# Two-layer trunk on one core: order of the state-space output products, of cross-attention's output halves, and of the first loads

## The chip, the cores and the metric

The kernel runs on one core of one Trainium2 chip. The metric is the device time of one execution in microseconds (us), the median of several. A core has TensorE (PE in the rows; PEld is its weight load), VectorE (DVE), ScalarE (ACT), GpSimd (POOL) and SyncE (SP). Each runs its own list of instructions in order and waits on the others by semaphores. SP only issues transfers here; ScalarE and GpSimd issue some in between their own work (ACTq and POOLq in rows).

## What is computed

A trunk of two layers over 512 positions of width 1024, with RMSNorm before each part and residual sums. Layer 0 mixes by stick-breaking attention and pooling (not touched here), layer 1 by a state-space layer; each layer then attends to 256 memory tokens in 4 heads and ends with a gated MLP. Cut to the two parts that the change moves:

```python
def s5_ssm(u, ...):                      # u = rmsnorm(x) @ ssm_w_in; 64 groups of 16 channels
    bu = einsum(ug, B)                   # 64 complex states per group
    h  = associative_scan(a, bu)         # h_t = a h_{t-1} + bu_t
    y  = Re(einsum(h, C))
    return y + d_skip * u                # then gelu, GLU, residual
def memory_cross_attention(h, mem_n, w_q, w_kv, w_o):
    q = h @ w_q;  k, v = split(mem_n @ w_kv)
    p = softmax(q k / 16)                # 4 heads of 256
    return (p v) @ w_o
```

## The kernel before

Activations stand transposed, as 8 tiles of 128 channels x 512 positions. Every large product is made exact to about float32 by splitting both sides into a high and a low part and adding three products, high x high, low x high and high x low (`mm3`, L207 to L209, or with the roles changed). Weights come as chunks of 256 KB (128 x 512) through a stream W: SP loads a raw chunk (`wr`, L168), ScalarE copies its high part (`wh`, L113), VectorE subtracts the low part (`wl`, L116). There are four buffers each. `W.take()` hands out a chunk and has the next ones converted, up to four in all, the one in use among them; so the two conversions of a chunk stand in the lists of ScalarE and VectorE where the chunk three places before it is taken.

The order of all engines around the change is written out by hand: each list holds the instructions in the order of the program's text.

**Start.** `x_block` loads x in four blocks of 256 columns (512 KB; the first in two halves); `W.load(n)` sees to it that n raw chunks are on their way. x tiles are then transposed one by one (`psx`, L217), normalised (xh on ScalarE L302, xl on VectorE L303), and one `v_step` of 12 matmuls (`psv`) follows each tile with the next chunk: W1 behind tile 2, W2 behind tile 3, W3 behind tile 4. cm is a block of constants; `columns()` reads it and the gain rows behind the last v_step.

**Cross-attention** (`xattn`, once a layer). `q_tile` makes a tile of q, `q_out` scales it and splits it (`xqh`, `xql`), `q_full` does both. `scores(h)` are two psum tiles of 12 matmuls with 256 columns (`pssc`) and the softmax; `turn(h)` transposes the probabilities (`pspt`), `values(h)` multiplies them by v (`pspv`). `o_first(m)` computes the first half of output tile m from the first two heads (`pso`, 12 matmuls, one chunk); NP says for how many tiles this is done early. The weight stream is put in the same order by `xattn_weights`.

**State space** (`ssm`, layer 1). Eight blocks b of 128 channels. Their steps are put in order by lists of names in `seq`:
- `um(b)` the input projection (24 matmuls, two chunks, `psu`); `uo(b)` scales it on VectorE (`su`) and ScalarE issues its store to DRAM (d_u); `sg(b)` is GpSimd's load of it in another layout; `lx(b)` and `ly(b)` GpSimd's loads of the block's matrices (wi, tb and wq, wo; 512 KB each).
- `x1(b)` the input products (8 float32 products of 64 columns, which the trace shows as 16 matmuls, `psX`), on ScalarE two half swaps `xs` and `mub`, on VectorE `sr`, `xs`, `sr` and the scan `gg`.
- `x2(b)` turns the states: two swaps `gsw` on ScalarE, then `gg`, `gsw` and `hb` on VectorE. hb has two buffers.
- `x3(b)` the output products (`psY`, 16 products, 32 matmuls in the trace: wq with sg, wo with hb), gelu on ScalarE (`sy`) and its store (d_y). `yl(b)` loads it back, `x4(b)` splits it (yh on ScalarE, yl on VectorE).
- between them stands work on the memory tokens for the cross-attention: `kk(m)`, a key tile of 48 matmuls with 256 columns in four chunks (`psk`, then kf, kh, kl), and `vs_(q)`, v-steps with two chunks (`psv`, weights wth and wtl).

All psum tiles of these parts come from one pool of eight banks. The order before is one block apart: x1(b), then x3(b-1).

Of the kernel before, what the change touches and what calls it, by code (L numbers as in the profile page):

```python
# [18 lines left out]
KD = D // 128  # L19
# [33 lines left out]
def trunk_kernel(  # L53
# [141 lines left out]
    W = Stream()  # L195
# [662 lines left out]
    def xattn_weights(layer):  # L858
        for m in range(KD):
            W.cols(xa_w_q[layer], m)  # L860
        for k0 in (0, 4):
            for m in range(3):
                W.cols(xa_w_o[layer], m, k0, 4)
        for m in range(3, KD):
            W.cols(xa_w_o[layer], m)


# [31 lines left out]
    kvm = KV(kv0)  # L899
# [15 lines left out]
    with tc.tile_pool(name="rg0", bufs=1, reuse_waits="tile") as rg, tc.manual_schedule():  # L915
# [9 lines left out]
        def x_block():  # L925
            c = len(xb)
            t = rg.tile([128, 4, 256], F32, tag="xb", bufs=4, name="xb")
            src = x[0, :, c * 256:(c + 1) * 256].rearrange("(i p) d -> p i d", p=128)
            if c == 0:
                nc.sync.dma_start(out=t[:, :, 0:128], in_=src[:, :, 0:128])  # L930
                W.load(1)
                nc.sync.dma_start(out=t[:, :, 128:256], in_=src[:, :, 128:256])
            else:
                nc.sync.dma_start(out=t, in_=src)
            xb.append(t)
# [5 lines left out]
        step(6)  # L941
        for c in range(4):
            x_block()
            W.load(c if c > 1 else 1)
        cm = rg.tile([128, C_W - C_K], F32, tag="cm", name="cm")
        nc.sync.dma_start(out=cm, in_=consts[:, C_K:C_W])
        for q in range(1, len(gl)):
# [312 lines left out]
    def xattn(rg, layer, norm, kv, nxt):  # L1260
# [13 lines left out]
        def q_out():  # L1274
            i = len(st["q"])
            f = np_.tile([128, 512], F32, tag="ev", bufs=2, name="qf")
            V.scalar_tensor_tensor(out=f, in0=ps_[i], scalar=1.0 / 16.0, in1=st["rbc"], op0=ALU.mult, op1=ALU.mult)
            a = rg.tile([128, 512], F32R, tag="xq", bufs=8, name="xqh")
            b = rg.tile([128, 512], F32R, tag="xq", bufs=8, name="xql")
            copy_hi(a, f)  # L1280
            sub_lo(b, f, a)
            st["q"].append((a, b))

        def q_full():
            q_tile()
            q_out()
# [47 lines left out]
                sub_lo(b, ps, a)  # L1334
                st["o"].append((a, b))

        NP = 3
        op = {}

        def o_first(m):  # L1340
            op[m] = psA("pso")
            sproj(op[m], st["o"][0:4], last=False)
# [3 lines left out]
        q_tile()  # L1346
        q_out()
        q_out()
        q_out()
        q_full()  # L1350
        scores(0)
        q_full()
        turn(0)
        scores(1)
# [5 lines left out]
        scores(2)  # L1360
        q_full()
        turn(2)
        scores(3)
        values(2)
        o_first(0)
        turn(3)
        o_first(1)
        values(3)
        o_first(2)
        for m in range(KD):  # L1370
            if m < NP:
                sproj(op[m], st["o"][4:8], first=False)
# [247 lines left out]
    def ssm(rg, norm, nxt, kvm):  # L1620
# [101 lines left out]
        with tc.manual_schedule():  # L1722
# [24 lines left out]
                for f in fs:  # L1747
                    f()

            seq(lx(0), kvm.load, um(0), st, um(1), row, uo(0), sg(0), uo(1), sg(1), lx(1), ly(0), um(2), ac(0), uo(2), sg(2), um(3), ac(1), ac(2), ac(3), lx(2), ly(1))  # L1750
            seq(x1(0), x2(0), uo(3), lx(3), ly(2))
            seq(x1(1), um(4), uo(4), x2(1), x3(0), lx(4), ly(3), sg(3), yl(0), kk(0))
            seq(x1(2), um(5), uo(5), x2(2), x3(1), ly(4), sg(4), kk(1), yl(1))
            seq(x1(3), um(6), uo(6), x2(3), x3(2), lx(5), yl(2), sg(5), kk(2))
            seq(x1(4), um(7), uo(7), x2(4), x3(3), lx(6), sg(6), x4(0), yl(3))
            seq(x1(5), ly(5), kk(3), vs_(0), x2(5), x3(4), ly(6), lx(7), sg(7), yl(4), x4(1), vs_(1))
            seq(x1(6), vs_(2), x2(6), x3(5), ly(7), yl(5), x4(2), x4(3), vs_(3))
            seq(x1(7), vs_(4), x2(7), x3(6), yl(6), vs_(5), x4(4), vs_(6), x3(7), yl(7), x4(5), vs_(7), x4(6))
            gps = []
            for i in range(NG1):  # L1760
                ps = psB("psg")
# [93 lines left out]
```

## Time and profile before

| | |
|---|---|
| time, median of 3 runs | 1507.06 us (1506.47 to 1507.28) |
| profiled execution, device time | 1506.5 us |
| its span in the trace | 1504.7 us |
| busy share of TensorE, VectorE, ScalarE, GpSimd | 98%, 68%, 49%, 28% |
| mean granted clock of TensorE | 0.994 |
| share of TensorE in the chain that ended last | 82% |

The span is from the first to the last instruction of the trace; the device time adds what lies around it. In the rows below a time stands first, from the span's start; "x4" counts like instructions in a row, whose duration is then that of all together; in brackets is the idle time of the engine before the row and the engine whose work ended it. The matmuls' ends are modelled, so the distance between two starts tells more than a duration. PEclk is the clock that TensorE was granted, as a share of the full 2.4 GHz.

### The profile page before, as it was taken

The page shows a single profiled execution, that of the slowest core. Times are in us where ns is not written, and L with a number is a line of the kernel's source. Part 1 is how long each engine was busy: PE and PEld are TensorE (multiplying, and loading weights), DVE is VectorE, ACT ScalarE, POOL GpSimd, SP SyncE. Part 2 cuts the span into 40 slices and gives each one's busy share as a digit, 9 for nine tenths or more (in the row PEclk, how much of TensorE's full clock was granted, in tenths as well). Part 3 has the DMA queues.
Part 4 walks back from the last instruction along what each step waited for, and adds up shares of the span by engine and source line. Part 5 has one row for each costly group of instructions (what it writes and reads, how often), then busy time and mean ns, then how long its engine had stood idle before and what let it go on. Part 6 is the DMA issues. An engine that isn't in the chain of part 4 may idle for free.

```text
span 1504.7 us, 21037 instructions
## 1 busy us (share of the span) xinstructions
PE 1480.7 (98%) x7347; PEld 1234.2 (82%) x7347; DVE 1023.4 (68%) x1586; ACT 733.5 (49%) x1303; POOL 420.5 (28%) x844
## 2 busy tenths in 40 slices
PE   8999999999999999999999999999999999999998
PEld 7787888888888887888788988888888888888887
DVE  4776666676588897888765666556667775377754
ACT  5556764344455534555663545434444543244533
POOL 7885429999000013333752120000000000000002
PEclk9999999999999999999999999999999999999999
DMA  6313243423433344444568876332133333333331
GB/s 184 96 46 96 74 142 99 118 92 107 124 100 105 109 158 135 133 121 129 154 187 306 263 252 194 105 102 70 56 92 91 99 93 96 100 98 98 92 118 56
DMA packets 271941, 183.99 MB, mean 122 GB/s; under 512 B 21271, under 2 KB 252763, under 8 KB 271835
## 3 DMA queue, kind: packets, MB, share of 16 engines
q1 hardware_dynamic: 244731, 132.79, 30.3%
q0 software_dynamic: 15872, 42.26, 8.4%
q10 hardware_dynamic: 11232, 7.61, 1.7%
q8 instruction: 57, 0.93, 0.3%
q14 instruction: 49, 0.40, 0.1%
HBM read 156.13 MB, written 24.12 MB: 120 GB/s over the span
## 4 chain that ended last, share of the span: by engine, by line
PE 82%; DVE 5%; issue 4%; POOL 3%; ACT 2%; DMA 2%; SPq 0%; ACTq 0%; DVEq 0%; POOLq 0%
PE psup L207 10%; PE psup L208 9%; PE psup L209 9%; PE psd L207 5%; PE psd L209 5%; PE psd L208 5%; PE pso L208 2%; PE pso L209 2%; PE pso L207 2%; PE psg L208 2%; PE psg L207 2%; PE psg L209 2%; PE psq L207 2%; PE psq L209 2%; PE psq L208 2%
## 5 line engine op out<-in xcount | busy, mean ns | idle before, releaser
L116 DVE TENSOR_TENSOR wl<-wr,wh 128x512 fp32r<-128x512 f32 (+2 forms) x467 | 325.3, 713 | 142.4 <-ACT wh L113 141.6
L113 ACT ACTIVATE wh<-wr 128x512 fp32r<-128x512 f32 (+2 forms) x467 | 280.4, 617 | 254.9 <-PE psup L208 84.5
L207 PE MATMUL psup<-xh,wh 128*128 128x512 f32 x704 | 275.7, 392 | 0.0
L208 PE MATMUL psup<-xl,wh 128*128 128x512 f32 x704 | 274.4, 390 | 0.0
L209 PE MATMUL psup<-xh,wl 128*128 128x512 f32 x704 | 274.1, 389 | 0.0
L1544 POOL TENSOR_TENSOR acc<-acc,sq 128x256 f32<-128x256 f32 x12 | 8.8, 735 | 558.4 <-ACT sq L1542 558.2
L207 PEld LDWEIGHTS psup<-xh,wh 128*128 128x128 f32 x704 | 132.1, 188 | 28.8 <-issue 1.5
L209 PEld LDWEIGHTS psup<-xh,wl 128*128 128x128 f32 x704 | 132.1, 188 | 28.2 <-DVE wl L116 0.3
L208 PEld LDWEIGHTS psup<-xl,wh 128*128 128x128 f32 x704 | 132.2, 188 | 27.1 <-issue 0.2
L207 PE MATMUL psd<-hh,wh 128*128 128x512 f32 x328 | 130.5, 398 | 0.2 <-ACT hh L113 0.2
L209 PE MATMUL psd<-hh,wl 128*128 128x512 f32 x328 | 128.2, 391 | 0.0
L208 PE MATMUL psd<-hl,wh 128*128 128x512 f32 x328 | 127.9, 390 | 0.2 <-DVE hl L116 0.2
L1458 ACT ACTIVATE fc<-fu,ccols 128x512 f32<-128x512 f32 x44 | 36.0, 818 | 93.7 <-DVE fu L1456 93.7
L302 ACT ACTIVATE xh<-xT,gcols 128x512 fp32r<-128x512 f32 x40 | 33.4, 835 | 97.1 <-DVE xT L325 68.9
L207 PEld LDWEIGHTS psd<-hh,wh 128*128 128x128 f32 x328 | 61.6, 188 | 14.8 <-issue 1.5
L209 PEld LDWEIGHTS psd<-hh,wl 128*128 128x128 f32 x328 | 61.5, 188 | 13.6
L208 PEld LDWEIGHTS psd<-hl,wh 128*128 128x128 f32 x328 | 61.6, 188 | 12.9 <-DVE hl L116 0.5
L715 POOL DMA_DIRECT2D tz<-kt x128 | 65.3, 518 | 7.4 <-POOL kt L712 4.7
L303 DVE SCALAR_TENSOR_TENSOR xl<-xT,gcols,xh 128x512 fp32r<-128x512 f32 x40 | 35.0, 874 | 33.6 <-ACT xh L302 33.5
L658 POOL DMA_DIRECT2D d_win<-wi x16 | 8.7, 546 | 155.5 <-ACT wi L655 155.5
L207 PE MATMUL psq<-xh,wh 128*128 128x512 f32 x128 | 51.1, 399 | 0.0
L1403 DVE TENSOR_TENSOR fu<-psup,rbc 128x512 f32<-128x512 f32 x44 | 30.3, 688 | 29.5 <-PE psup L209 28.2
(352 smaller groups left out, 3500.6 us busy)
## 6 DMA issues: line engine op xcount, KB each, us to landing
wr<-in_ffn_w_up_dram SPq DMA_DIRECT2D x176, 256.0 KB, 2.9
wr<-in_ffn_w_down_dram SPq DMA_DIRECT2D x70, 256.0 KB, 2.9
wr<-in_xa_w_kv_dram SPq DMA_DIRECT2D x64, 256.0 KB, 4.5
wr<-in_ab_w_in_dram SPq DMA_DIRECT2D x32, 256.0 KB, 2.9
wr<-in_xa_w_q_dram SPq DMA_DIRECT2D x32, 256.0 KB, 2.9
wr<-in_xa_w_o_dram SPq DMA_DIRECT2D x32, 256.0 KB, 2.8
wr<-in_ssm_w_glu_dram SPq DMA_DIRECT2D x29, 256.0 KB, 2.8
wr<-in_ffn_w_down_dram SPq DMA_DIRECT2D x24, 192.0 KB, 2.6
```

The costliest lines, as they stand in the source:

```text
L113: A.activation(out=o, in_=i, func=AF.Copy)
L116: V.tensor_tensor(out=o, in0=i, in1=hi.bitcast(F32), op=ALU.subtract)
L207: T.matmul(ps, lhsT=lh, rhs=rh, start=first, stop=False)
L208: T.matmul(ps, lhsT=lh, rhs=rl, start=False, stop=False)
L209: T.matmul(ps, lhsT=ll, rhs=rh, start=False, stop=last)
L302: A.activation(out=ho, in_=src, func=AF.Copy, scale=g)
L303: V.scalar_tensor_tensor(out=lo, in0=src, scalar=g, in1=ho.bitcast(F32), op0=ALU.mult, op1=ALU.subtract)
L658: nc.gpsimd.dma_start(out=d_win[b // 2][:, (b % 2) * 512:(b % 2) * 512 + 512], in_=st["w"])
L715: nc.gpsimd.dma_start(out=tzs[b % 2][j:128:8, :, j * 16:128], in_=ktf[:, :, 0:128 - j * 16])
L1403: V.tensor_tensor(out=u, in0=ps, in1=rbc, op=ALU.mult)
L1458: A.activation(out=c, in_=u, func=AF.Identity, scale=cwcol(layer, 2, t), bias=cbcol(layer, t))
L1544: G.tensor_tensor(out=acc[:, sl], in0=acc[:, sl], in1=sq[:, 0:256], op=ALU.add)
```

## The change

Three parts are changed, all of them orders. At the start two chunks more are asked for early: W1 goes ahead of x1, W2 ahead of x2, W3 ahead of x3, and W4 behind it. In cross-attention NP becomes 4, with the weight stream to match; the third q_out moves behind the first scores, and the first o_first stands ahead of the last scores. In the state-space part x3(b-2) stands behind x1(b), um(4) goes between the first two x1, key tile 0 follows x1(1), key tiles 1 to 3 follow um(5) to um(7), and the v-steps stand one place earlier.

```diff
-            for m in range(3):
+            for m in range(4):
                 W.cols(xa_w_o[layer], m, k0, 4)
-        for m in range(3, KD):
+        for m in range(4, KD):
             W.cols(xa_w_o[layer], m)
...
                 W.load(1)
                 nc.sync.dma_start(out=t[:, :, 128:256], in_=src[:, :, 128:256])
+                W.load(2)
...
             x_block()
-            W.load(c if c > 1 else 1)
+            W.load(c + 2 if c < 3 else 4)
...
-        NP = 3
+        NP = 4
...
         q_out()
         q_out()
-        q_out()
         q_full()
         scores(0)
+        q_out()
...
         turn(2)
+        o_first(0)
         scores(3)
         values(2)
-        o_first(0)
+        o_first(1)
         turn(3)
-        o_first(1)
+        o_first(2)
         values(3)
-        o_first(2)
+        o_first(3)
...
-            seq(lx(0), kvm.load, um(0), st, um(1), row, uo(0), sg(0), uo(1), sg(1), lx(1), ly(0), um(2), ac(0), uo(2), sg(2), um(3), ac(1), ac(2), ac(3), lx(2), ly(1))
-            seq(x1(0), x2(0), uo(3), lx(3), ly(2))
-            seq(x1(1), um(4), uo(4), x2(1), x3(0), lx(4), ly(3), sg(3), yl(0), kk(0))
-            seq(x1(2), um(5), uo(5), x2(2), x3(1), ly(4), sg(4), kk(1), yl(1))
-            seq(x1(3), um(6), uo(6), x2(3), x3(2), lx(5), yl(2), sg(5), kk(2))
-            seq(x1(4), um(7), uo(7), x2(4), x3(3), lx(6), sg(6), x4(0), yl(3))
-            seq(x1(5), ly(5), kk(3), vs_(0), x2(5), x3(4), ly(6), lx(7), sg(7), yl(4), x4(1), vs_(1))
-            seq(x1(6), vs_(2), x2(6), x3(5), ly(7), yl(5), x4(2), x4(3), vs_(3))
-            seq(x1(7), vs_(4), x2(7), x3(6), yl(6), vs_(5), x4(4), vs_(6), x3(7), yl(7), x4(5), vs_(7), x4(6))
+            seq(lx(0), kvm.load, um(0), st, um(1), row, uo(0), sg(0), uo(1), sg(1), lx(1), ly(0), um(2), ac(0), uo(2), sg(2), um(3), ac(1), ac(2), ac(3), lx(2))
+            seq(x1(0), um(4), uo(3), x2(0), ly(1), uo(4), lx(3))
+            seq(x1(1), kk(0), x2(1), ly(2), lx(4))
+            seq(x1(2), x3(0), sg(3), um(5), uo(5), x2(2), ly(3), yl(0), kk(1))
+            seq(x1(3), x3(1), sg(4), um(6), uo(6), x2(3), ly(4), lx(5), yl(1), kk(2))
+            seq(x1(4), x3(2), sg(5), um(7), uo(7), x2(4), lx(6), yl(2), x4(0), kk(3))
+            seq(x1(5), x3(3), sg(6), vs_(0), x2(5), ly(5), lx(7), yl(3), x4(1), vs_(1), vs_(2))
+            seq(x1(6), x3(4), sg(7), vs_(3), x2(6), ly(6), yl(4), x4(2), vs_(4), x4(3))
+            seq(x1(7), x3(5), vs_(5), x2(7), ly(7), yl(5), x3(6), x4(4), yl(6), vs_(6), x3(7), yl(7), x4(5), vs_(7), x4(6))
```

**SP at the start of the program, before** (xb are the x blocks, wr the weight chunks W0, W1, W2, cm constants; the number behind a name tells buffers apart):

```order
L937 DMA cs_76<-in_consts_dram 128x192
L930 DMA xb_232<-in_x_dram 128x4x128
L168 DMA wr_234<-in_ab_w_in_dram 128x512
L932 DMA xb_232<-in_x_dram 128x4x128
L934 DMA xb_237<-in_x_dram 128x4x256
L934 DMA xb_239<-in_x_dram 128x4x256
L168 DMA wr_241<-in_ab_w_in_dram 128x512
L934 DMA xb_243<-in_x_dram 128x4x256
L168 DMA wr_245<-in_ab_w_in_dram 128x512
L946 DMA cm_247<-in_consts_dram 128x640
```

The same place after:

```order
L938 DMA cs_76<-in_consts_dram 128x192
L930 DMA xb_232<-in_x_dram 128x4x128
L168 DMA wr_234<-in_ab_w_in_dram 128x512
L932 DMA xb_232<-in_x_dram 128x4x128
L168 DMA wr_237<-in_ab_w_in_dram 128x512
L935 DMA xb_239<-in_x_dram 128x4x256
L168 DMA wr_241<-in_ab_w_in_dram 128x512
L935 DMA xb_243<-in_x_dram 128x4x256
L168 DMA wr_245<-in_ab_w_in_dram 128x512
L935 DMA xb_247<-in_x_dram 128x4x256
L947 DMA cm_249<-in_consts_dram 128x640
```

W1 stood behind x2 and W2 behind x3, W3 behind all that is shown; now a chunk goes ahead of each of the blocks x1, x2 and x3.

**TensorE in the cross-attention of layer 0, where the last head's scores begin, before** (pspt are the transposes of turn(2), pssc the scores):

```order
L217 MATMUL pspt_4156<-cs_76,p_4076 128x128 x2
L217 MATMUL pspt_4156<-cs_76,p_4095 128x128 x2
L207 MATMUL pssc_4165<-kh_1896,xqh_4034 128x256
L208 MATMUL pssc_4165<-kl_1897,xqh_4034 128x256
L209 MATMUL pssc_4165<-kh_1896,xql_4035 128x256
```

After (pso is the first half of output tile 0; its 12 matmuls begin behind the same transposes, the last three are shown):

```order
L207 MATMUL pso_4165<-oh_4056,wh_4014 128x512
L208 MATMUL pso_4165<-ol_4057,wh_4014 128x512
L209 MATMUL pso_4165<-oh_4056,wl_4015 128x512
L207 MATMUL pssc_4184<-kh_1896,xqh_4034 128x256
L208 MATMUL pssc_4184<-kl_1897,xqh_4034 128x256
L209 MATMUL pssc_4184<-kh_1896,xql_4035 128x256
```

A first half of the output, which came behind values(2), now stands between turn(2) and the scores.

**VectorE in the state-space part, before: from x2(0) to su(4)** (the first three rows are x2(0), the su rows uo(3) and uo(4), the four rows behind the first su x1(1); the wl rows are the low parts of key tile 0's second and third chunk):

```order
L1693 TENSOR_TENSOR gg_8661<-gg_8661,tb_8386 128x512
L1694 TENSOR_TENSOR gsw_8663<-gsw_8663,tb_8386 128x512
L1695 TENSOR_TENSOR hb_8376<-gg_8661,gsw_8663 128x8x64
L1660 TENSOR_TENSOR su_8669<-psu_8564,rbc_8491 128x512
L1679 TENSOR_TENSOR sr_8693<-psX_8680,tb_8505 128x512
L1680 TENSOR_TENSOR xs_8689<-xs_8689,tb_8505 128x512
L1681 TENSOR_TENSOR sr_8693<-sr_8693,xs_8689 128x512
L1683 SCALAR_TENSOR_TENSOR gg_8697<-mub_8378,sr_8693 128x512
L116 TENSOR_TENSOR wl_8701<-wr_8534,wh_8700 128x512
L116 TENSOR_TENSOR wl_8719<-wr_8569,wh_8718 128x512
L1660 TENSOR_TENSOR su_8736<-psu_8699,rbc_8491 128x512
```

VectorE after, from the same place, behind the scan of x1(0); the last row, wl_8737, is the low part of key tile 0's fourth chunk:

```order
L116 TENSOR_TENSOR wl_8661<-wr_8534,wh_8660 128x512
L116 TENSOR_TENSOR wl_8679<-wr_8569,wh_8678 128x512
L1662 TENSOR_TENSOR su_8696<-psu_8564,rbc_8491 128x512
L1695 TENSOR_TENSOR gg_8657<-gg_8657,tb_8386 128x512
L1696 TENSOR_TENSOR gsw_8699<-gsw_8699,tb_8386 128x512
L1697 TENSOR_TENSOR hb_8376<-gg_8657,gsw_8699 128x8x64
L1662 TENSOR_TENSOR su_8709<-psu_8659,rbc_8491 128x512
L1681 TENSOR_TENSOR sr_8729<-psX_8716,tb_8505 128x512
L1682 TENSOR_TENSOR xs_8725<-xs_8725,tb_8505 128x512
L1683 TENSOR_TENSOR sr_8729<-sr_8729,xs_8725 128x512
L1685 SCALAR_TENSOR_TENSOR gg_8733<-mub_8378,sr_8729 128x512
L116 TENSOR_TENSOR wl_8737<-wr_8587,wh_8736 128x512
```

x1(1) (sr, xs, sr, gg) stays behind su, but two low parts and both su now stand ahead of it, and the low part that key tile 0 reads last stands behind its scan; before, that key tile came behind um(4) and x3(0).

**TensorE at block 1 of the state-space part, before** (psX are the input products of blocks 0 and 1, psu is um(4)):

```order
L1673 MATMUL psX_8644<-sg_8496,wi_8384 128x64 x8
L1673 MATMUL psX_8680<-sg_8501,wi_8503 128x64 x8
L207 MATMUL psu_8699<-xh_7769,wh_8530 128x512
L208 MATMUL psu_8699<-xl_7770,wh_8530 128x512
L209 MATMUL psu_8699<-xh_7769,wl_8531 128x512
```

After (psu is the end of um(4), psk key tile 0):

```order
L207 MATMUL psu_8659<-xh_8353,wh_8565 128x512
L208 MATMUL psu_8659<-xl_8354,wh_8565 128x512
L209 MATMUL psu_8659<-xh_8353,wl_8566 128x512
L1675 MATMUL psX_8716<-sg_8501,wi_8503 128x64 x8
L207 MATMUL psk_8735<-mem_8553,wh_8583 128x256
L208 MATMUL psk_8735<-mem_8553,wh_8583 128x256
L209 MATMUL psk_8735<-mem_8553,wl_8584 128x256
```

um(4) moved between the two input products, and key tile 0 follows the second of them directly.

## Rows read from the trace of the kernel before

**Rows 1.** TensorE's waits, state-space part (800:960 us): engine, line, releaser: us, times, longest.

```profile
PE psY L1705 <- issue: 2.4, 1, 2.4
PE psv L207 <- ACT wth L113: 1.0, 1, 1.0
PE psk L207 <- ACT wh L113: 1.0, 1, 1.0
PE psk L209 <- DVE wl L116: 0.9, 2, 0.6
PE psv L208 <- DVE wtl L116: 0.5, 1, 0.5
```

**Rows 2.** Windows: us, busy (count) of PE, PEld, DVE, ACT, POOL, PEclk, DMA, GB/s.

```profile
4.00:12.00 8.00, 5.86 (x33) 4.38 (x32) 2.37 (x4) 2.20 (x4) 3.22 (x16) 1.00 0.93 299
819.80:826.50 6.70, 6.70 (x33) 6.70 (x33) 4.99 (x7) 2.80 (x6) 0.43 (x1) 0.50 1.03 394
```

**Rows 3.** TensorE's timeline in the state-space part, blocks 0 to 2.

```profile
806.87 3.68 PE L1673 MATMUL psX<-sg,wi 128*128 128x64 f32 x32
...
818.67 0.41 PE L1705 MATMUL psY<-hb,wo 128*128 128x64 f32 x2 [2.41 <-issue]
...
832.72 1.90 PE L1673 MATMUL psX<-sg,wi 128*128 128x64 f32 x16
834.43 0.48 PE L207 MATMUL psu<-xh,wh 128*128 128x512 f32 x1
...
840.00 0.33 PE L1704 MATMUL psY<-sg,wq 128*128 128x64 f32 x2
...
843.49 0.36 PE L207 MATMUL psk<-mem,wh 128*128 128x256 f32 x1
...
849.33 1.89 PE L1673 MATMUL psX<-sg,wi 128*128 128x64 f32 x16
```

**Rows 4.** TensorE's timeline at the start: start, us, engine, line, operation [idle before <-releaser].

```profile
10.67 0.60 PE L217 MATMUL psx<-cs,xb 128*128 128x128 f32 x4
12.48 0.50 PE L207 MATMUL psv<-wh,xh 128*128 128x512 f32 x1 [1.21 <-ACT wh L113]
15.84 0.60 PE L217 MATMUL psx<-cs,xb 128*128 128x128 f32 x4
19.06 0.60 PE L217 MATMUL psx<-cs,xb 128*128 128x128 f32 x4
23.25 0.60 PE L217 MATMUL psx<-cs,xb 128*128 128x128 f32 x4
```

**Rows 5.** ScalarE's timeline, same stretch: the copies of two weight chunks.

```profile
11.80 0.63 ACT L113 ACTIVATE wh<-wr 128x512 fp32r<-128x512 f32 x1 [1.63 <-DMA wr<-in_ab_w_in_dram]
18.75 0.63 ACT L113 ACTIVATE wh<-wr 128x512 fp32r<-128x512 f32 x1 [4.16 <-DMA wr<-in_ab_w_in_dram]
```

**Rows 6.** VectorE's timeline, the same blocks.

```profile
811.78 0.69 DVE L1679 TENSOR_TENSOR sr<-psX,tb 128x512 f32<-128x512 f32 x1 [0.74 <-ACT xs L1676]
...
816.55 0.69 DVE L1693 TENSOR_TENSOR gg<-gg,tb 128x512 f32<-128x512 f32 x1 [1.33 <-ACT gsw L1692]
...
820.85 0.69 DVE L1679 TENSOR_TENSOR sr<-psX,tb 128x512 f32<-128x512 f32 x1 [1.69 <-ACT xs L1676]
...
824.10 1.27 DVE L116 TENSOR_TENSOR wl<-wr,wh 128x512 fp32r<-128x512 f32 x2
...
827.68 0.69 DVE L1693 TENSOR_TENSOR gg<-gg,tb 128x512 f32<-128x512 f32 x1 [1.71 <-ACT gsw L1692]
```

**Rows 7.** TensorE's timeline in cross-attention: scores(3), values(2); in layer 1 scores(3).

```profile
333.42 0.36 PE L207 MATMUL pssc<-kh,xqh 128*128 128x256 f32 x1
...
337.33 0.40 PE L207 MATMUL pspv<-pth,vh 128*128 128x512 f32 x1
...
1077.85 0.39 PE L209 MATMUL pssc<-kh,xql 128*128 128x256 f32 x1 [0.22 <-DVE xql L116]
```

**Rows 8.** ScalarE's timeline where the v-steps' chunks are copied.

```profile
890.50 0.63 ACT L113 ACTIVATE wth<-wr 128x512 fp32r<-128x512 f32 x1 [7.88 <-DMA wr<-in_xa_w_kv_dram]
```

## The prediction

> **What bounds the kernel now.** TensorE works nearly without a break, so I read its waits first, in the whole run and then by stage. What the change can win back is there: idle time of TensorE, the time in which its pipeline refills, and the time at the lower clock. The start has two such places, the cross-attentions one each, the state-space part five [rows 1]: the output products of block 0 wait 2.4 us (for hb, though the row says issue), key tile 0 waits 1.0 us for a weight's high part and, with key tile 3, 0.9 us for low parts, a v-step 1.0 and 0.5 us. Together 5.8 us. Behind the longest of them the granted clock is 0.50 for 6.7 us [rows 2], which is the 1.2 GHz level: half of that, 3.4 us, is lost. TensorE had been idle for 2.4 us before [rows 3]. Everything that the change doesn't name keeps its order, and TensorE goes on from one stage to the next without slack, so what a stage wins or loses I carry to the end one to one.
>
> **Start: weights ahead of x.** The transposes of x tiles 2 to 5 (two a block) begin at 10.67, 15.84, 19.06 and 23.25 [rows 4]: the three stretches between are 5.17, 3.22 and 4.19 us long and hold the same work, a tile's transposes and one v_step with chunks W1, W2 and W3, so 1.95 and 0.97 us are lost. In the first, the matmul waits 1.21 us for the copy of chunk W1; the copy itself started at 11.80 after ScalarE had waited 1.63 us for the transfer [rows 5]. In the third ScalarE has waited 4.16 us for W3 and starts at 18.75 [rows 5], and the x copies behind it are late by that. Now W1 leaves ahead of x1 and x2, 1 MB. At the 299 GB/s of this stretch [rows 2] that is 3.5 us, so W1 lands near 8.3 instead of just before 11.8, and it is wanted at 10.67. W3, which stood behind x3, cm and the gain rows, now goes ahead of x3 and is earlier by several us; both waits go. What is next late is the low part of W1, which VectorE subtracts behind the low part of the x block: between nothing and one such operation, 0.64 us (half of the 1.27 us of two [rows 6]); I take 0.35. Gain 1.95 + 0.97 - 0.35 = **2.6 us**, bounds 1.9 and 2.9. The price is on the x blocks: each comes one chunk, 256 KB or 0.9 us, later. x2 and x3 are wanted at 19.06 and after 23.25, long after; but no row tells how long x1 had lain there when it was taken at 10.67 (rival D). cm and the gain rows are later too; columns() reads them only behind the last of these stretches.
>
> **Cross-attention.** The 24 matmuls of the last head's scores take from 333.42 to 337.33, 3.91 us [rows 7]. A key tile's 48 matmuls of the same form take 843.49 to 849.33, 5.84 us [rows 3], so 24 want 2.92. The 0.99 us are waits for the q tile that was finished last and its low part. One first half of the output (12 matmuls of 512 columns; 24 of them are the 5.57 us from 834.43 to 840.00 [rows 3], so 2.8 us) now stands ahead of these scores and covers it. The fourth first half moves 12 matmuls from the end to here and adds nothing to their sum; its pso bank is one of eight. Two layers: 2.0 us. The third q_out moved behind the first scores lets turn(0) come at the same time as now, since the DVE chain to it is unchanged; I allow 0.2 us more. Gain **2.2 us**, bounds 1.2 (if one layer's wait only moves) and 2.6.
>
> **State space: what goes.** With x3 two blocks behind x1, hb is ready long before it is read: 2.4 us go. The waits of key tiles 0 and 3 and of the v-step (3.4 us) are all of this part's old order and go as well. A wait costs more than its idle time: in the first stretch of the start 1.95 us are lost and 1.21 us of idle stand in its largest row, so some 0.3 us for each further step. Five waits: 1.4 us. The clock: 3.4 us. Removed: 5.8 + 1.4 + 3.4 = 10.6 us.
>
> **State space: what comes.** Key tile 0 now follows block 1's input products directly. Its chunks 2 and 3 are converted while um(4) runs, but the low part of its fourth chunk stands on VectorE behind the whole chain of x1(1), and the high part on ScalarE behind the swaps (xs) of x1(1), which stand behind the store of su(4). I follow VectorE's list in the new order with the lengths of the old [rows 6]. sr of block 0 starts at 811.78, as now, since what releases it is unchanged. From an sr to the operation behind its scan are 3.25 us (820.85 to 824.10): 815.03. Two low parts, su(3), its store, the two swaps on ScalarE and the start of gg: 3.58 us (824.10 to 827.68): 818.6. gg, gsw, hb, su and then sr of block 1: 4.30 us (816.55 to 820.85): 822.9. Again 3.25 us: 826.2; the low part itself 0.64: **826.8**. TensorE meanwhile [rows 3]: input products at 806.87, 1.71 us for 16 (832.72 to 834.43), um(4) 5.57, input products 1.71: key tile 0 begins at 815.9. Three chunks of 1.46 us (5.84 / 4) bring it to 820.2, where it wants the fourth. It idles 3.9 us until the high part is there (near 824.1), does two matmuls and idles on until 826.8: **6.5 us**. This is one wait where before there were two, 2.4 and 1.2 us long, at the same blocks.
>
> Key tiles 1 and 2 follow their um directly too. Their fourth chunk comes behind su (3.58 less two low parts, 2.3 us after um's end), gg, gsw and hb (3 x 0.64) and itself (0.64): 4.9 us after um's end, wanted after 4.4. With the latency between engines 0.6 us each. Key tile 3 has the low part of x4(0) as well, 1.2 us. The v-steps that are now bunched earlier (two in a row in the row of block 5) want their chunks earlier: now ScalarE waits 7.88 us for such a chunk's transfer [rows 8], so they are not lying ready. Between 0 and 4 us; I take 1.8, nearer to the waits of 1.0 and 0.5 that this place has now. Together 6.5 + 0.6 + 0.6 + 1.2 + 1.8 = 10.7, refilling 5 x 0.2 = 1.0.
>
> The clock: now it falls at 819.80, 3.5 us after the idle time began (818.67 less 2.41), and is back at 826.50. After the change the idle time begins at 820.2 and is longer and in two pieces. Set off by the same time, the low stretch lies from 823.8 to 830.4, and TensorE works in it from 826.8 on: 3.6 us at half speed lose 1.8. If it lies wholly behind the wait, 3.4. I take 2.2, nearer the first, since it is the row's own distance.
>
> The Trainium skill, page "TensorE: Matmul & The Clock Gate", section "Why this matters for your kernels", advises against long idle gaps between bursts of matmuls, since the clock goes back to its lower level after them; that speaks against this change, which makes one long gap out of two short ones. The trace agrees that a gap of 2.4 us was followed by the lower level. Charged in full by that rule the sum would be 1.2 us worse, 1506.7.
>
> State space: +10.7 + 1.0 + 2.2 - 10.6 = **+3.3 us**, bounds: without the v-steps' and the clock's share -0.7, with 4 us of the one and 3.4 of the other +6.7.
>
> **Sum.** -2.6 - 2.2 + 3.3 = -1.5 us. The profiled execution took 1506.5 us with a span of 1504.7; the median is 1507.06, so the profile stands 0.6 us below. From the median: 1505.5 us.
>
> **The rivals.** A difference of 0.2%, 3.0 us (1504.05 and 1510.07), is about what a measurement can tell here from no change.
> Forecast: the new wait eats most of what the rest wins. 1504.1 to 1508.0.
> B, faster: the wait at key tile 0 is short or the clock doesn't fall. Against it speaks that VectorE and ScalarE take their lists in order; for it, that the clock's fall and the v-steps are my guesses. Without clock and v-steps 1505.5 - 2.2 - 2.0 = 1501.3; if the fourth chunk came 3 us sooner besides, 1498.
> C, slower: the v-steps' chunks collide with the 512 KB loads of wi, tb, wq and wo that GpSimd issues there; TensorE then waits 4 us instead of 1.8 and the clock falls a second time (3.4): 1505.5 + 2.2 + 3.4 = 1511. It decides from a wait at that place as long as the 2.4 us that brought the clock down before. For it speaks the 7.88 us row, against it that TensorE lost only 1.5 us there.
> D, the start doesn't do what it says: x1 comes late instead of W1. If it had landed only just in time, it is late by W1's 0.9 us, or 1.8 where W1 and x1 share the queues: the gain falls from 2.6 to 0.8, 1507.3. Against it speaks that its transposes show no wait.
>
> **How the numbers follow.** Forecast 0.56, B 0.29, C 0.08, D 0.07. Predicted 1505.5. The range leaves out C's 1511 and the outer third of B: 1501.2 to 1508.3. Faster by over 0.2%: B, 0.29. Slower: C, 0.08. Within: forecast and D, 0.63. The likeliest case's own range is 1504.1 to 1508.0.
>
> **What would show it.** At the start: stretches between the transposes near 3.2 to 3.6 us, no ScalarE wait for W1 or W3. Cross-attention: no wait in the last scores, their stage near 2.9 us. State space: no psY wait; a psk wait of about 4 us for a high part and 2.5 for a low one, near 815 to 822 on the new run's clock; a stretch at 0.50 over it and behind it; short psk waits on low parts at the other tiles. The prediction is wrong if key tile 0 runs through without a wait, if the granted clock stays at 1.00 there, or if a wait of several us turns up among the v-steps.

## The result, and the profile after

| | before | after |
|---|---|---|
| time, median | 1507.2 us | 1523.35 us (1519.38 to 1524.74, 4 runs) |
| ratio | | 1.0106 (1.0092 to 1.0119) |
| profiled execution, device time | 1506.5 us | 1524.7 us |
| its span | 1504.7 us | 1523.0 us |
| mean granted clock of TensorE | 0.994 | 0.984 |

The change makes the kernel 16 us slower. The forecast was 1505.5 us, with a range up to 1508.3: wrong in sign and size. The profiled execution is the slowest of the four, so the profiles differ by 18.3 us where the medians differ by 16.2. The start of the same matmul in both traces tells what each part did to the time (in us from the span's start; a part's share is how much the distance between the two traces grows in it):

| part, up to | before | after | its share | forecast |
|---|---|---|---|---|
| start, and the rest before cross-attention | 288.04 | 289.19 | +1.15 | -2.6 |
| cross-attention, layer 0 | 400.03 | 399.46 | -1.7 | -1.1 |
| MLP, layer 0 | 794.37 | 793.46 | -0.3 | 0 |
| state space | 1032.55 | 1050.57 | +18.9 | +3.3 |
| cross-attention, layer 1 | 1141.43 | 1159.70 | +0.25 | -1.1 |
| end of the span | 1504.7 | 1523.0 | 0 | 0 |

TensorE's waits of after from the state-space part to the end, without one of 0.2 us (columns as in [rows 1]):

```profile
PE psk L209 <- DVE wl L116: 4.6, 4, 2.3
PE psk L207 <- ACT wh L113: 3.8, 1, 3.8
PE psv L207 <- ACT wth L113: 2.2, 1, 2.2
PE psv L208 <- DVE wtl L116: 1.6, 1, 1.6
PE psup L207 <- DVE xT L325: 0.9, 1, 0.9
PE psq L207 <- DVE sig L1783: 0.9, 1, 0.9
```

The psY wait that headed [rows 1] is gone. In its place stand the announced waits of key tile 0, for a high part (3.8) and for a low part (the 2.3 among the four psk waits on wl), a longer wait at a v-step (2.2 and 1.6), and two short ones that I had not named. The waits alone are no 18.9 us. The windows show the rest (columns as in [rows 2]: PE, PEld, DVE, ACT, POOL, PEclk, DMA, GB/s); the first is the idle time at key tile 0:

```profile
819.30:826.10 6.80, 0.73 (x5) 0.33 (x3) 4.99 (x8) 3.99 (x7) 2.09 (x4) 0.83 1.05 393
824.00:840.80 16.80, 14.73 (x64) 14.25 (x65) 10.28 (x16) 7.11 (x11) 2.48 (x4) 0.50 0.62 204
902.50:919.20 16.70, 15.37 (x60) 14.30 (x61) 7.27 (x12) 4.24 (x8) 2.62 (x5) 0.50 0.44 134
```

TensorE is granted 0.50 twice in the state-space part, 17 us each time, and works through most of both stretches; before there was one of 6.7 us there [rows 2]. Half of 14.73 and of 15.37 us is 15 us lost. TensorE's timeline at the two places:

```profile
819.21 0.28 PE L209 MATMUL psk<-mem,wl 128*128 128x256 f32 x1
823.29 0.39 PE L207 MATMUL psk<-mem,wh 128*128 128x256 f32 x1 [3.80 <-ACT wh L113]
826.07 0.58 PE L209 MATMUL psk<-mem,wl 128*128 128x256 f32 x1 [2.27 <-DVE wl L116]
...
901.68 0.50 PE L207 MATMUL psv<-wth,mem 128*128 128x512 f32 x1 [2.20 <-ACT wth L113]
903.84 0.79 PE L208 MATMUL psv<-wtl,mem 128*128 128x512 f32 x1 [1.65 <-DVE wtl L116]
```

Why the high part comes late at key tile 0 stands in ScalarE's timeline:

```profile
820.45 0.33 ACTq L1663 DMA_DIRECT2D d_u<-su  x1
820.87 0.59 ACT L1677 ACTIVATE xs<-psX 64x512 f32<-64x512 f32 x1 [3.11 <-DVE su L1662]
822.62 1.65 ACT L113 ACTIVATE wh<-wr 128x512 fp32r<-128x512 f32 x3
```

ScalarE stood 3.11 us behind VectorE's su(4), whose store it issues at 820.45; then came the swaps of x1(1), and then the copy at 822.62 that TensorE wanted at 819.5. Ahead of the v-step, ScalarE's timeline again:

```profile
899.19 0.63 ACT L1693 ACTIVATE gsw<-gg 64x512 f32<-64x512 f32 x1 [2.28 <-DVE gg L1685]
900.48 0.63 ACT L113 ACTIVATE yh<-yf 128x512 fp32r<-128x512 f32 x1
901.02 0.61 ACT L113 ACTIVATE wth<-wr 128x512 fp32r<-128x512 f32 x1
```

The chunk's copy, wth, waits for no transfer there. It stands behind the swaps of x2(5), which wait 2.28 us for VectorE's scan, and behind yh of x4(1).

### The profile page after: what moved, and what is told of

Its sections match the earlier page's. It is cut to its first block, busy times and chain, and to the rows that moved or that the text cites. A ratio compares the mean times of both kernels' runs of the same rounds, so it can differ in the third digit from the quotient of the medians.

```text
span 1523.0 us, 21037 instructions
## 1 busy us (share of the span) xinstructions
PE 1493.0 (98%) x7347; PEld 1245.3 (82%) x7347; DVE 1019.5 (67%) x1586; ACT 733.7 (48%) x1303; POOL 422.1 (28%) x844
## 4 chain that ended last, share of the span: by engine, by line
PE 91%; DVE 3%; DMA 2%; issue 1%; ACT 1%; SPq 0%; POOL 0%; DVEq 0%; POOLq 0%; ACTq 0%
PE psup L207 10%; PE psup L208 10%; PE psup L209 10%; PE psd L207 5%; PE psd L209 5%; PE psd L208 5%; PE pso L208 2%; PE pso L209 2%; PE pso L207 2%; PE psq L207 2%; PE psq L209 2%; PE psq L208 2%; PE psg L209 2%; PE psg L208 2%; PE psg L207 2%
## 5 line engine op out<-in xcount | busy, mean ns | idle before, releaser
L207 PE MATMUL pso<-oh,wh 128*128 128x512 f32 x128 | 50.2, 392 | 0.0
```

What stands on the lines that cost most here:

```text
L207: T.matmul(ps, lhsT=lh, rhs=rh, start=first, stop=False)
```

## Experiments

**One part at a time.** Three kernels, each the kernel before with one part of the change: the start (the lines with W.load), the cross-attention (NP, the weight order, q_out and o_first), the state-space lists.

> Only the start part of the change (two more chunks asked for ahead of the x blocks). Theory: the gain at tile 2 is given back at tile 5, where ScalarE copies the chunks W4 and W5, which land late behind the gain rows on SP, ahead of the tile's xh; in the trace of the change the program was 1.7 us behind at 43 us and 1.15 us behind from 170 to 288 us. So 1.1 us slower: 1508.3, with a wait of 1.4 us of a psv matmul for xh near 23 us. Rival, the prediction: 2.6 us faster, 1504.6.

> Only the cross-attention part. Theory: 1.7 us faster in layer 0 and nothing in layer 1, where a wait of 1.0 us for a psum bank at the first matmul behind it (psup for xT) takes the gain: 1505.4. Rival, the prediction: 2.2 us faster in sum and no wait at psup: 1504.9; second rival, the bank's wait belongs to the state-space part's count of psum tiles, then it is missing here and layer 1 gains 1.0 too: 1504.4.

> Only the state-space part. Theory: all of the loss is here: waits of 6.4 us at key tile 0 and 4.2 us at the v-steps, and two stretches of the granted clock at 0.50 of some 17 us each, together 18 us slower: 1525. Rival: the three parts disturb one another (the shifted transfers of the start), and this part alone gives the predicted 3.3 us: 1510.5, with one short stretch at 0.50.

| part alone | us | before beside it | ratio (95%) |
|---|---|---|---|
| start | 1506.4 | 1506.8 | 0.9996 (0.9986 to 1.0005) |
| cross-attention | 1505.4 | 1506.8 | 0.9991 (0.9981 to 1.0001) |
| state space | 1522.3 | 1506.8 | 1.0095 (1.0063 to 1.0127) |

The whole loss is in the state-space lists. The 1.4 us of the cross-attention are at the edge of what can be told: its interval just includes no change. The start gives nothing that can be told from noise. Its trace says why; TensorE's timeline with the start part alone:

```profile
11.08 0.66 PE L217 MATMUL psx<-cs,xb 128*128 128x128 f32 x4
14.41 0.60 PE L217 MATMUL psx<-cs,xb 128*128 128x128 f32 x4
17.61 0.60 PE L217 MATMUL psx<-cs,xb 128*128 128x128 f32 x4
22.02 0.66 PE L217 MATMUL psx<-cs,xb 128*128 128x128 f32 x4 [1.04 <-ACT xT L974]
```

The first stretch is 3.33 us instead of 5.17 [rows 4], as forecast, but the third, from 17.61 on, is 4.41 and the fourth 4.90 us long (the next transposes begin at 26.92, before at 26.45). The gain of the first is given back there. ScalarE at that place:

```profile
20.85 0.63 ACT L113 ACTIVATE wh<-wr 128x512 fp32r<-128x512 f32 x1 [5.11 <-DMA wr<-in_ab_w_in_dram]
21.39 0.58 ACT L974 ACTIVATE xT<-psx 128x512 f32<-128x512 f32 x1
```

It waits 5.11 us for the transfer of W4, and the copy of x (xT) that the transposes at 22.02 wait for stands behind that. W4 leaves late because SP issues cm and nine loads of rows ahead of it; SP's own timeline in the trace of after:

```profile
6.75 1.95 SPq L947 DMA_DIRECT2D cm<-in_consts_dram  x1
...
16.63 7.20 SPq L168 DMA_DIRECT2D wr<-in_ab_w_in_dram  x6
```

So the change does not ask for W4 behind x3, as was said ahead of the prediction: `W.load(4)` wants four chunks on their way, these are W0 to W3, and cm follows x3. In the profiled execution of after the clock fell here as well, as this window shows:

```profile
25.10:28.50 3.40, 3.40 (x12) 2.61 (x11) 1.62 (x3) 3.31 (x12) 2.82 (x8) 0.50 0.41 121
```

TensorE works in all of these 3.4 us, so 1.7 us are lost. Neither before nor the start part alone has a low stretch at this place.

**Is it the idle time that brings the clock down?** The change with extra products of 512 columns where TensorE idled: 26 (5.9 us) ahead of key tile 0's fourth chunk, 17 ahead of the late chunk of vs_(2). They go into the psum tile that the next input products overwrite.

```diff
+                    sproj(ps[:, MEM:2 * MEM], self.ma[0:4], MEM, last=False)
+                    self.fill(pad)
+                    sproj(ps[:, MEM:2 * MEM], self.ma[4:8], MEM, first=False)
...
+                    if n == 2 and half == 0 and k == 5:
+                        self.fill(17)
...
+            kk = lambda q: (lambda: kvm.k(q, 26 if q == 0 else 0))
```

> The changed kernel with idle time of TensorE filled: 26 extra products of 512 columns (0.23 us each, 5.9 us, written to a psum tile that is overwritten later) ahead of key tile 0's fourth chunk, and 17 (3.9 us) ahead of the sixth v-chunk. Theory, the idle time brings the clock down: the granted clock stays at 1.00 in the state-space part, the waits take as long as before, and the time falls by the 15 us that the two stretches at half speed cost, to 1508.5. Rival, the clock falls by what the part does there (transfers, the mix of products) or the waits themselves are the loss: the stretches at 0.50 stay and the time stays near 1523.

1510.42 us, ratio to before 1.0025 (1.0016 to 1.0035): 12.9 us less than after. The windows of the same two places:

```profile
819.30:826.10 6.80, 6.37 (x30) 5.13 (x29) 4.99 (x8) 3.37 (x6) 2.03 (x4) 1.00 1.05 394
824.00:840.80 16.80, 16.37 (x113) 14.98 (x112) 12.01 (x18) 8.96 (x15) 2.49 (x4) 1.00 0.96 303
```

113 matmuls in the 16.8 us where after has 64. The conversions come no sooner, yet the state-space part takes 243.0 us instead of 257.1: 14.1 us are the clock's. The first window's DMA share (1.05) and all lists are those of after, so it is neither contention nor the order of the conversions. What is left in this part, 243.0 us against 238.2 of before, is the order's own cost in waits, now filled; the 238.2 us still hold the low stretch of before.

**How much idle time?** Two kernels that leave only a piece of key tile 0's idle time and fill the rest: 16 products ahead of the chunk (a last piece of 2.4 us stays), or 10 between its first products and the first low part (the first piece, 4.0 us, stays). The v-step is filled in both. Each was measured in one execution only.

```diff
-            kk = lambda q: (lambda: kvm.k(q, 26 if q == 0 else 0))
+            kk = lambda q: (lambda: kvm.k(q, 16 if q == 0 else 0))
```

> The changed kernel with only the first piece of key tile 0's wait filled (16 extra products, 3.65 us) and the v-steps' wait filled as in the run with all fills; left is one idle piece of some 2.4 us, for the low part, as long as the psY wait of the kernel before. What sets the length of the stretch at 0.50? Theory A, the idle time ahead of it: a short single piece brings a stretch of 6.7 us as before, and some 3 us on the time of the filled run, 1513.5. Theory B, the work that follows at this place: 17 us, 7.4 us on the time, 1518. Theory C: a single piece behind busy work doesn't bring the clock down at all, 1510.4.

> The changed kernel with only the second piece filled: TensorE idles 4.0 us until the high part of key tile 0's fourth chunk, then the 2.3 us until its low part are filled with 10 extra products, and the v-steps' wait is filled. Theory A, a longer single piece brings a longer stretch at 0.50: between 6.7 and 17 us, time 1514 to 1518. Theory B, the following work sets it: 17 us, 1518. Theory D, the second idle piece, which lies in the slow stretch, renews it: without it 6.7 us, and 1513.5.

With the 2.4 us piece 1518.4 us, with the 4.0 us piece 1514.1 us. First the one with 2.4 us:

```profile
824.00:826.40 2.40, 0.13 (x2) 0.00 (x0) 2.31 (x4) 0.72 (x2) 0.00 (x0) 1.00 1.03 410
826.40:842.70 16.30, 16.30 (x117) 15.32 (x118) 10.14 (x16) 8.74 (x14) 2.49 (x4) 1.00 0.76 235
846.00:859.90 13.90, 13.90 (x61) 13.32 (x61) 6.58 (x9) 4.92 (x8) 3.04 (x5) 0.51 0.47 128
```

then the one with 4.0 us (behind this window the clock is 1.00 again):

```profile
822.50:829.30 6.80, 5.09 (x14) 4.12 (x15) 5.59 (x8) 3.31 (x6) 0.00 (x0) 0.51 1.06 403
```

One piece of 4.0 us brings a low stretch of 6.8 us; both pieces together brought 17. But 2.4 us idle brought none at its place, where before the same length was followed by one [rows 2, 3], and a later pair of waits, 0.4 and 1.7 us at key tile 1 by starts (the distance between two starts less one matmul's time), brought 13.6 us. Theory D fits the second kernel (6.8 us, 1514.1 against 1513.5), theory A only with the lower end of its range; none fits the first: theory B's 1518 us came out by luck, by a stretch at another place. So the length of the low stretch is not read off the length of one idle piece, and no theory that I had put down holds for both.

**The same fill in the kernel before.** Ten extra products ahead of the psY that waits in [rows 3].

```diff
+            if b == 0:
+                for _ in range(10):
+                    T.matmul(py, lhsT=kvm.ma[7][0][:, 0:128], rhs=kvm.mt, start=True, stop=True)
```

> The kernel before with 10 extra products (2.3 us) ahead of block 0's output products, so that TensorE has no idle time while it waits for hb. Theory, the idle time brings the clock down: no stretch at 0.50 near 820 us, 3.4 us faster, 1503.4. Rival, the stretch comes from something else there (the transfers run at over 390 GB/s): it stays, 1506.8.

1508.18 us, ratio 1.0012 (0.9996 to 1.0029): no gain. The psY wait is gone, but key tile 0 now waits; its row of TensorE's waits:

```profile
PE psk L207 <- ACT wh L113: 3.0, 1, 3.0
```

The clock falls behind that instead, as the window shows:

```profile
831.50:835.50 4.00, 3.40 (x15) 3.17 (x16) 2.63 (x5) 2.11 (x4) 1.65 (x3) 0.57 0.94 267
```

ScalarE's copies that key tile 0 wants, in before:

```profile
830.01 2.19 ACT L113 ACTIVATE wh<-wr 128x512 fp32r<-128x512 f32 x4 [0.46 <-ACT sy L1707]
```

and here:

```profile
831.42 2.19 ACT L113 ACTIVATE wh<-wr 128x512 fp32r<-128x512 f32 x4 [0.46 <-ACT sy L1711]
```

They start 1.41 us later here, and the psY that had waited does so by 1.40 (820.07 instead of 818.67), so the lists stand as they did and the products only took the place of the wait. What changed is the clock behind it: TensorE came to key tile 0's last chunk about 2 us sooner against these copies, and waited for them 3.0 us instead of 1.0 [rows 1]. So in before the low stretch had covered a late conversion; the time it cost was no time to be won by itself.

**Another order of the same lists.** If the conversions stand too far back on VectorE and ScalarE, x1's vector part behind um and su and x2 behind the key tile should mend it. In the kernel before, x1 is split into its products and a part e1 for the rest:

```diff
+            seq(x1(0), e1(0), um(4), uo(3), x2(0), ly(1), lx(3))
+            seq(x1(1), kk(0), uo(4), e1(1), x2(1), ly(2), lx(4))
+            seq(x1(2), x3(0), sg(3), um(5), e1(2), ly(3), yl(0), kk(1), uo(5), x2(2))
```

> The kernel before with another order of the state-space part: output products two blocks behind as in the change, but the vector and scalar steps of x1(b) come behind the um of their block, and su and x2 behind the key tile, so that no chunk's conversion stands behind a block's chain where TensorE wants it; key tile 0 comes ahead of su(4) and x1(1)'s chain. Theory, the change's loss is the place of the conversions in the lists of VectorE and ScalarE: key tile 0 waits 0.2 to 0.5 us, the v-steps under 1, the granted clock stays at 1.00, and the five old waits and the old slow stretch are gone too: 1506.8 - 7.2 - 3.4 + 2 = 1498. Rival, the distance of two blocks itself is the trouble (the work is bunched and the wait comes up at another chunk, with a slow stretch): 1507 or more.

1516.53 us, ratio 1.0064 (1.0046 to 1.0081). Key tile 0 waits 0.9 us by starts only, but key tile 1 waits 6.4 us for a high part, until 841.43. ScalarE's timeline:

```profile
824.40 0.63 ACT L113 ACTIVATE wh<-wr 128x512 fp32r<-128x512 f32 x1 [4.63 <-DMA wr<-in_ssm_w_in_dram]
827.80 0.63 ACT L113 ACTIVATE wh<-wr 128x512 fp32r<-128x512 f32 x1 [2.77 <-DMA wr<-in_xa_w_kv_dram]
...
840.74 1.15 ACT L113 ACTIVATE wh<-wr 128x512 fp32r<-128x512 f32 x2 [0.46 <-ACT sy L1714]
```

The copy that TensorE wants is the last row. It waits for no transfer itself; it stands behind the scalar steps of x1(1), x2(1) and x3(0). But ahead of these ScalarE had stood 4.63 and 2.77 us for the transfers of two other chunks, and VectorE, which subtracts their low parts, behind it. The window of that time:

```profile
811.00:830.00 19.00, 18.24 (x136) 17.14 (x135) 10.17 (x15) 6.20 (x12) 5.41 (x10) 1.00 0.96 333
```

The DMA engines are full (0.96, 333 GB/s) with GpSimd's loads of the blocks' matrices, 512 KB each; a 256 KB chunk issued at 816.34 landed only at 827.7. Next, the same order with these loads one or two blocks later (only the first rows are shown):

```diff
-            seq(x1(0), e1(0), um(4), uo(3), x2(0), ly(1), lx(3))
+            seq(x1(0), e1(0), um(4), uo(3), x2(0))
...
-            seq(x1(2), x3(0), sg(3), um(5), e1(2), ly(3), yl(0), kk(1), uo(5), x2(2))
+            seq(x1(2), x3(0), sg(3), um(5), e1(2), ly(1), lx(3), yl(0), kk(1), uo(5), x2(2))
```

> The reordered state-space part of the run before (conversions ahead of the blocks' chains), with GpSimd's 1 MB loads of wq, wo and wi, tb for blocks 1 to 4 moved some 15 us later, behind sg(3). There, key tile 1 waited 6.4 us for a chunk whose transfer took over 11 us beside these loads. Theory, the transfers bound this place once the lists no longer do: with the loads later the chunks land some 3 us after their issue, the wait at key tile 1 falls under 1 us, no slow stretch there, and the time is 1500 to 1503. Rival, the wait has another cause (the length of VectorE's and ScalarE's lists in these blocks): key tile 1 waits over 4 us again, 1514.

1520.14 us, ratio 1.0095 (1.0063 to 1.0127): slower again. The same window:

```profile
811.00:830.00 19.00, 18.25 (x136) 17.15 (x135) 14.16 (x21) 7.81 (x14) 3.78 (x8) 1.00 0.62 192
```

the same copies on ScalarE:

```profile
834.00 1.15 ACT L113 ACTIVATE wh<-wr 128x512 fp32r<-128x512 f32 x2 [0.46 <-ACT sy L1714]
```

and TensorE's longest waits from 790 to 960 us:

```profile
PE psX L1673 <- issue: 5.9, 1, 5.9
PE psk L209 <- DVE wl L116: 3.4, 4, 1.9
```

The DMA share falls to 0.62, the copies start 6.7 us earlier in the same list, and key tile 1 waits 0.3 us for its high part. So the transfers had put that list back. But the input products of block 7 now wait 5.9 us. The row doesn't name for what; GpSimd issued the load of their matrix wi at 900.22, the longest of these loads took 9.3 us to land, and they start at 909.61. The clock falls behind that, to 0.50 for 17 us. The collision was real; moving all loads moved the wait.

**The start mended, with the cross-attention part.** In the kernel before, both parts of the change, and cm and the rows issued only behind the chunks up to W7:

```diff
+            W.load(c + 2 if c < 3 else 4)
...
+        def late_rows():
+            nc.sync.dma_start(out=cm, in_=consts[:, C_K:C_W])
...
             W.fill()
+            if m == 3:
+                late_rows()
```

> The kernel before with the start and the cross-attention part of the change, and one thing mended at the start: the transfers of cm and of the gain and convolution rows are issued by SP behind the chunks W4 to W7 instead of ahead of them. Theory, the gain at the start was given back because SP's row transfers hold up W4 and W5, whose copies stand on ScalarE ahead of tile 5's xh: the stretches between the transposes of tiles 2 to 7 are 3.2 to 3.7 us each, the start gains 2.6 us, cross-attention 1.4 as alone, together 1502.8. Rival, W4 and W5 come late for another reason (the buffers or the x blocks ahead of them): tile 5 waits as before, and 1505.2.

1503.0 us, ratio 0.9967 (0.9957 to 0.9977). TensorE at the start:

```profile
10.87 0.60 PE L217 MATMUL psx<-cs,xb 128*128 128x128 f32 x4
14.43 0.60 PE L217 MATMUL psx<-cs,xb 128*128 128x128 f32 x4
17.64 0.60 PE L217 MATMUL psx<-cs,xb 128*128 128x128 f32 x4
20.83 0.60 PE L217 MATMUL psx<-cs,xb 128*128 128x128 f32 x4
```

Every stretch is 3.2 to 3.6 us, as the prediction wanted them, and the late W4 is gone: it was SP's list. A product of the next stage (psqk) that starts at 41.90 in before starts at 39.49 here, 2.4 us earlier, close to the 2.6 of the forecast.

**All three, with the state-space part in a third order; and the mended kernel with three first halves.** The third order is the second with e1(5) behind vs_(1) and some of the matrices loaded earlier again. The other kernel takes back NP = 4 and its fourth first half, and keeps the rest:

```diff
-        NP = 4
+        NP = 3
...
         values(2)
-        o_first(1)
         turn(3)
-        o_first(2)
+        o_first(1)
         values(3)
-        o_first(3)
+        o_first(2)
```

> The mended start and the cross-attention part (together 1503.0 alone) with a third order of the state-space part: conversions ahead of the blocks' chains, GpSimd's loads of blocks 1 to 4 later, those of blocks 5 to 7 early again, and x1(5)'s chain behind the second pair of v-steps. In the second order x1(7) waited 5.9 us for its matrices and the v-steps 2.3 us, and behind them the clock fell for 17 us (8.5 us lost). Theory, these are the last late arrivals: no wait over 2.5 us in the part, no slow stretch, the part 2 us shorter than that of the kernel before: 1501. Rival, each order only moves the late arrival to another place, since transfers, ScalarE and VectorE are close to their limit in this part: another wait over 3 us with a slow stretch, 1508 or more.

> The mended start, and of the cross-attention part only the moves, with three first halves of the output instead of four. Theory, the fourth half cost a psum bank: with it, the next part's first matmul (psup) waits 1.0 us in layer 1 for the bank of the last output tile; without it that wait goes, but turn(3) follows values(2) directly and waits for the softmax of the last head, about 1 us a layer: 1503.0 - 1.0 + 2.0 = 1504. Rival, turn(3) doesn't wait: 1502.0.

The third order took 1521.06 us, ratio 1.0103 (1.0086 to 1.012). Its two longest waits, 280 to 1160 us:

```profile
PE psv L207 <- ACT wth L113: 3.1, 1, 3.1
PE psk L207 <- ACT wh L113: 2.8, 1, 2.8
```

The waits moved once more. Four orders with x3 two blocks behind x1 were slower than before, each through late operands of its own; whether one exists that wins stays open.

The kernel with three first halves took 1500.91 us (1500.48 to 1501.74), ratio 0.9961 (0.9946 to 0.9976), which beats both kernels. Its waits in the same window are nearly those of [rows 1]:

```profile
PE psY L1710 <- issue: 2.4, 1, 2.4
PE psk L209 <- DVE wl L116: 0.6, 1, 0.6
```

The rest of its rows are 0.5 us or less. The psup wait, 0.9 us in the kernel with four halves, is gone, and layer 1's cross-attention takes 107.97 us where before it took 108.88 and after 109.13. So the wait came with the fourth first half, and turn(3) needs no cover: no row shows it waiting. The two kernels' intervals overlap; whether three halves beat four in the total is not shown.

## Why the prediction was wrong, step by step

**The clock in the state-space part: this term failed most.** I took 2.2 us, at most 3.4, by giving the new low stretch the length of the old one, 6.7 us. It was 17 us, and there were two; filling the idle time took 14.1 us away. The mechanism, a low stretch set off by the idle time, was right; the length was taken from one row as if it were fixed, and the runs show that it isn't. The sentence on the Trainium skill ("TensorE: Matmul & The Clock Gate", section "Why this matters for your kernels") pointed the right way: idle gaps between matmuls are what brought the lower level, and the traces agree, since with the gaps filled the part stays at 1.00; the price was far above the 1.2 us by which I had charged it. But that one long gap is dearer than two short ones is not what the traces show: 4.0 us in one piece brought 6.8 us at the lower level, 2.2 and 1.65 brought 17. Rival C asked for a second fall of the clock behind the v-steps; that came, at the place and from waits that are together above its 2.4 us, and I gave it 0.08. Its cause, late transfers, did not come, and its 1511 us were still 12 short. The stated 1508.0 was also less than the working allows: with its own upper bound for the state-space part, +6.7, the sum is 1508.9.

**The v-step: 4.3 us by starts, forecast 1.8 with a bound of 4.** I looked for late transfers, from [rows 8]. ScalarE did not wait for the chunk; its copy stood behind x2(5) and x4(1) there, its low part behind the same blocks on VectorE. The lists were in the order of the change; I had followed them at key tile 0 only.

**The start: -2.6 forecast, +1.15 found.** The step "what is next late is the low part of W1" failed. W1 to W3 came as forecast, but ScalarE then waited for W4, which SP issues behind cm and nine loads of rows. I had written that these are read late and costed them at nothing; what counted was what SP issues behind them. The mended start shows it. In the trace of after 1.7 us more went to the low clock from 25.1 to 28.5 us, which the forecast for the start did not contain.

**The banks.** "Its pso bank is one of eight" was wrong in layer 1: the first psup product waits 0.9 us for VectorE's xT, the last reader of a psum tile; with three first halves the wait is gone, so the fourth brought it. A psq wait of 0.9 us for VectorE's sig stands at the end of the state-space part; it is there with that part alone too, and that it is for a bank is inferred from the reader. About 1.8 us that I had at nothing.

**What was right.** Key tile 0 idled 6.4 us by starts, in two pieces of 4.0 and 2.4, where 6.5 in 3.9 and 2.6 was forecast: following VectorE's list row by row with the durations of [rows 6] gave it. Key tiles 1 and 2 waited 0.73 each and key tile 3 1.33, forecast 0.6, 0.6 and 1.2. The waits of the old order went. The last head's scores in layer 0 took 2.87 us, forecast 2.92: they begin at 336.65, and the next product, a pspv, at 339.52.

**The ledger of the state-space part.** Waits 6.4 + 0.7 + 0.7 + 1.3 + 4.3 + 0.9 = 14.3 instead of 11.7, and the clock 14.1 instead of 2.2; less the 10.6 removed, that is 17.8 of the 18.9 found. The forecast's own sum was uneven in a small term: about 0.3 us of refilling beside each old wait, 0.2 beside each new one, which is 0.4 us over five waits.

## What to carry to other kernels

When TensorE is the bound, price an idle gap by the low clock that may follow it, and give that price a wide range: here waits of 6.4 and 4.3 us cost 14.1 us more by the clock. A second row of before would not have helped: its other low stretch, in layer 0, is as long as the first. Before moving work on TensorE, follow the lists of the engines that prepare its operands at every place that moves, and the list of the queue that issues the transfers too. If a gap can't be avoided, products with no use in it were cheaper here than the clock, but first look what is wanted next: the time won can go into a wait for an operand that is late there.

## What the runs showed of the hardware

The low stretch was longer than I expected and not settled by the idle time ahead of it. The same wait in two kernels shows it best: psY in block 0 waits 2.4 us in before and in the mended kernel with three first halves, and in layer 0's attention, which no kernel changes, a product (psm) waits 1.6 us in the one and 1.5 in the other. Windows of the low stretches behind these waits, first before:

```profile
154.20:161.00 6.80, 5.80 (x21) 4.67 (x21) 3.90 (x9) 3.94 (x9) 2.62 (x3) 0.50 0.00 0
819.80:826.60 6.80, 6.80 (x34) 6.80 (x34) 4.99 (x7) 2.90 (x6) 0.43 (x1) 0.50 1.02 392
```

then the mended kernel:

```profile
149.70:159.90 10.20, 10.20 (x41) 8.49 (x40) 4.70 (x10) 7.25 (x19) 3.20 (x3) 0.50 0.07 25
815.30:825.50 10.20, 10.20 (x50) 10.20 (x50) 6.65 (x11) 5.53 (x9) 1.34 (x3) 0.50 1.00 369
```

Elsewhere I found 3.4 us at the granted 0.50 behind a wait of 3.0 us (the fill in the kernel before), 6.8 behind 4.0, 10.2 behind 6.4 (the first of the other orders), 17 behind 3.8 and 2.3 and 20.5 behind 3.8 and 2.0 (the state-space part alone), 17 behind 2.2 and 1.65, 17 behind 5.9, 13.6 behind 0.4 and 1.7, none behind 2.4 in the half-filled kernel. TensorE was busy for 60 to 100% of these stretches, in the mended kernel for all of both, so being busy again did not end them at once. What sets the length stays open. It also varies from one execution to the next: four of the state-space part alone took 1514.4 to 1526.7 us, at mean clocks of 0.993 down to 0.984, while ten of the filled kernel lay within 1509.3 to 1511.3.

A transfer of 256 KB, whose median from issue to landing is 2.7 to 5.0 us in after, depending on the weight, took 11.4 us beside GpSimd's loads at a DMA share of 0.96.
